# A two-layer decoder trunk on one core: first tiles and first weight chunk in smaller parts, identity made on chip

## The chip, the cores and the metric

The kernel runs on one core of one Trainium2 chip. The metric is device time in microseconds of one execution. Engines: TensorE (PE; PEld is its weight load), VectorE (DVE), ScalarE (ACT), GpSimd (POOL), SyncE (SP, which here only issues DMAs).

## The reference

Two layers work on 256 tokens of 1024 numbers, all in float32. Of each layer only the beginning matters here:

```python
def rmsnorm(x, g):
    xf = x.astype(jnp.float32)
    y = xf * lax.rsqrt(jnp.mean(xf * xf, axis=-1, keepdims=True) + EPS)
    return (y * g.astype(jnp.float32)).astype(x.dtype)
...
    h = rmsnorm(x, mix_norm)
    z = h @ w_in
...
    g = jax.nn.sigmoid((h @ w_branch_gate).astype(jnp.float32)).astype(x.dtype)
```

`z` goes to three token mixers (sparse, sliding-window and latent attention, with rotary tables made from the positions); their outputs are weighted by the gates, merged and multiplied by `w_out`; a gated feed-forward part of 2816 columns and a gated embedding part follow. After the second layer comes a last norm.

## The kernel before

The tokens are two tiles `t` of 128. A multiplication, `lin(name)`, takes the transposed tokens as the stationary and 512 columns of weights as the moving operand. For accuracy each float32 operand is split into a rounded part (high) and a residual (low), and each contraction step of 128 rows makes three products into one bank of PSUM: high x high, high x low, low x high. Weights come in chunks of two contraction steps (512 KB). A chunk is loaded by SyncE into one of four `raw` buffers, rounded by ScalarE into `wh` (the cast `wh<-raw`), and VectorE makes the residual `wl`; there are six pairs of `wh` and `wl`. `upper` issues the cast, its inner `rest` the residual and then the load of the chunk four further on.

The first multiplication of layer 0 is `gc0` (gate columns of mixer C, chunks 0 to 3), the second `g1` (chunks 4 to 7). `gc0` goes through its eight contraction steps in blocks of two, tile 0 then tile 1 in each block; `g1` makes all eight steps of tile 0, then those of tile 1. The two banks of `gc0` are read by ScalarE as gates, `gateC = tanh(z * rh)`, where `rh` is half the inverse root of the mean square of the tile's tokens, computed on GpSimd from sums that ScalarE makes (`junk<-x`, the squares).

The split tokens `hT` are made so: four 128x128 transposes on TensorE (`tr<-con,x`, with the identity in the constants `con`), a product with the norm's gain on VectorE (`xg<-tr,lp`, the gain in the loaded parameters `lp`), the rounding on ScalarE (`hT<-xg`), the residual on VectorE. `parts(t, g)` does this for tile `t` and half `g` of the 1024 features. Warm-up products on a tile of ones (`pv<-wrm`, counts in `WARM`) stand between.

The order on each engine is that of issue in the program. Most of it is set by a planner, `W`, that keeps estimated times of the engines and takes waiting pieces of work from a queue by due time; `feed` issues casts and residuals of coming chunks by these estimates. The first steps are written out by hand at the end of `build`, and `script[t, k]` puts pieces of them ahead of step `k` of tile `t` of `gc0`. The program builds the rotary tables on the side: GpSimd reduces the angles (`kq`, `kp`, `ang`), VectorE makes one step (`kq<-kq,ang`), ScalarE evaluates sines, for which it loads another function table (`ACT_TABLE_LOAD`) and afterwards the one with tanh again.

Each DMA counts on one of eight semaphores in turn, and the order below names them (`DMAHW0` is the load of `con`).

Of the kernel before, what the change touches and what calls it, by code (L numbers as in the profile page):

```python
# [8 lines left out]
F32 = mybir.dt.float32  # L9
F32R = mybir.dt.float32r  # L10
BF16 = mybir.dt.bfloat16
I32 = mybir.dt.int32
AF = mybir.ActivationFunctionType
# [49 lines left out]
LEAD, GAP = 128, 256  # L63


C_ID, C_FREQ, C_FIRST = 0, 128, 176
C_CB, C_CM, C_MV, C_S, C_J, C_N = 0, 32, 64, 192, 224, 228
C_BAND, C_CAUS, C_ALL = 0, 128, 256

# [148 lines left out]
def build(tc, wst, xin, pin, posn, cst, lpar, fnorm, out):  # L218
# [34 lines left out]
    def load_to(n):  # L253
        while st["dma"] < min(n, len(CHUNKS)):
            i = st["dma"]
            off, kk, c = CHUNKS[i]
            r = sb([P, 1024], name="raw", bufs=RAWB, p=wp)
            nc.sync.dma_start(out=r[:, :kk * c],
                              in_=wst[off:off + P * kk * c].rearrange("(p n) -> p n", p=P))
            W.op("D", kk * c * P * 4 / 350e3, [r.tensor.name], [])  # L260
            W.end[r.tensor.name] = ("D", W.t["D"] + 2.0)
            raws[i] = r
            st["dma"] += 1
# [67 lines left out]
    def lin(l, name, nk, lhs, evac, blocks=None, wait=0.0, halves=False):  # L331
# [5 lines left out]
        for b in blocks:  # L337
            for t in range(2):
                if t and halves:
                    break  # L340
                for k in range(k0, k0 + b):
                    for fn in script.pop((t, k), ()):
                        fn()
                    i, wh, wl = wtile(l, name, k)
                    xh, xl = lhs(t, k)
                    o = banks[t][:, :c]
                    T.matmul(out=o, lhsT=xh, rhs=wh, start=(k == 0), stop=False)
                    T.matmul(out=o, lhsT=xh, rhs=wl, start=False, stop=False)
                    T.matmul(out=o, lhsT=xl, rhs=wh, start=False, stop=(k == nk - 1))
                    if k == nk - 1:  # L350
                        evac(t, banks[t])
                    if t == 1 and (k % kp == kp - 1 or k == nk - 1):
                        done(i, wait if k0 + b == nk else 0.0)
                    W.tick()
            k0 += b
# [20 lines left out]

    x = [[sb([P, 512], name=f"x{t}{g}") for g in range(2)] for t in range(2)]
    con = sb([P, C_FIRST], name="con")
    con2 = sb([P, C_N], name="con2")
    pos = sb([P, 2], I32, name="pos")  # L380
    lps = {}
# [15 lines left out]
    mload = sb([P, 2, P], name="mload", tag="kall", bufs=3)  # L397
    load(nc.gpsimd, mload, cst[:, C_FIRST + C_N:].rearrange("p (a b) -> p a b", a=2))
    load(nc.gpsimd, con2, cst[:, C_FIRST:C_FIRST + C_N])
    ident = con[:, C_ID:C_ID + P]  # L400
    identb = sb([P, P], BF16, name="identb")
    identr = sb([P, P], F32R, name="identr")
    masks = sb([P, 2, P], BF16, name="masks")
# [861 lines left out]
        return n4  # L1265


    nm = Norm(lps[0][:, L_MIX:L_MIX + 8])
    wrm = sb([P, 512], BF16, name="wrm", tag="junk")
    V.memset(wrm, 1.0)  # L1270
    wps = ps("pv")
# [24 lines left out]
    def split(i):  # L1296
# [2 lines left out]
            upper(i)  # L1299
        return late.get(i, lambda: None)  # L1300

    def start_1():
        nm.square(0, 0)
        nm.square(1, 0)
        w2 = split(2)
        lo = parts(0, 1)
        w2()
        lo()

    def start_2():  # L1310
        w3 = split(3)
        lo = parts(1, 1)
        w3()
        lo()
        w4 = split(4)
        nm.square(0, 1)
        w4()
# [2 lines left out]
        W.push([], setup_masks, 20.0)  # L1320
        split_to(HLB)

    warm(WARM[0])
    lo = parts(0, 0)
    w0 = split(0)
    lo()
    warm(WARM[1])
    lo = parts(1, 0)
    w0()
    warm(WARM[2])  # L1330
    w1 = split(1)
    lo()
    w1()
    script[1, 0] = [start_1]
    script[0, 2] = [start_2]
    for l in range(DEPTH):
        nm = layer(l, nm, None)
    W.until(lambda: len(sent) == 2)
# [3 lines left out]
SPACE = 4.4  # L1342
SLACK = 0.9
TWO = "ga"
WARM = (7, 4, 4)
NEAR = 2
WAIT = 1.5

# [1 line left out]
def host_layout(inputs):  # L1350
# [47 lines left out]
    lp = np.ascontiguousarray(np.stack(lp))  # L1398
    i = np.arange(P)
    con, con2, con3 = (np.zeros((P, n), np.float32) for n in (C_FIRST, C_N, C_ALL))  # L1400
    con[:, C_ID:C_ID + P] = np.eye(P)
    con3[:, C_CAUS:C_CAUS + P] = np.where(i[None, :] <= i[:, None], 0, NEG)
    con3[:, C_BAND:C_BAND + P] = np.where(i[None, :] > i[:, None], 0, NEG)
    fr = [10000.0 ** (-np.arange(0, d, 2) / d) for d in (64, 32)]
# [34 lines left out]
```

## Time and profile before

| | |
|---|---|
| median of 3 runs | 967.37 us (967.33 to 967.55) |
| the profiled execution | 968.79 us, of which 967.0 us is the span from the first to the last instruction |
| instructions | 13566 |
| mean granted TensorE clock | 0.997 of 2.4 GHz |

The page gives each engine's busy time as a share of the span. Matmuls are pipelined, and the end of each is modelled, so that a product's printed duration is longer than the distance to the next one. A row's "idle" is the time in which the engine did nothing ahead of the instruction, and the name behind the arrow is what ended it. All times are microseconds from the span's start unless marked ns. Almost every instruction carries line 214, the helper through which the program issues; so rows are told apart by their tiles.

### The profile page before, as it was taken

Reading aid. Unit: us, or ns where it says so; the run is one execution under the profiler, and the core shown is the slowest. Engines: PE = TensorE matmul, PEld = TensorE weight load, DVE = VectorE, ACT = ScalarE, POOL = GpSimd, SP = SyncE. Lnnn points to the kernel's source line nnn. Section 1 sums busy time; section 2 is a strip of 40 time slices with the busy share of each in tenths; the row PEclk is TensorE's granted clock in tenths of the full one; section 3 lists DMA queues with packets and bytes.
Section 4 is the critical chain, followed back from the end, with each engine's and each line's share of the span. In section 5 each row is a group of like instructions: output and inputs, shape, how many; then the busy total and the mean of one; then the engine's idle time right before and its main releaser. Section 6 shows DMA issues by size and latency. Waiting matters only on the chain.

```text
span 967.0 us, 13566 instructions
## 1 busy us (share of the span) xinstructions
PE 954.5 (99%) x4915; PEld 785.3 (81%) x4915; DVE 665.5 (69%) x1044; ACT 555.2 (57%) x1013; POOL 51.0 (5%) x101
## 2 busy tenths in 40 slices
PE   8999999999999999999999999999999999999996
PEld 5888887777888888888888898877788888888886
DVE  6696798668776666655767868866786766666554
ACT  6668766565554445443665686666655544444444
POOL 7200000000010000000121000000000000000010
PEclk9999999999999999999999999999999999999999
DMA  8556534424555555656454664443444555555551
GB/s 281 163 164 227 182 110 153 152 87 162 175 184 186 199 182 175 196 174 209 158 173 156 201 204 142 131 153 131 131 139 167 194 189 193 192 189 180 190 175 44
DMA packets 46595, 164.29 MB, mean 170 GB/s; under 512 B 5504, under 2 KB 5760, under 8 KB 46528
## 3 DMA queue, kind: packets, MB, share of 16 engines
q1 hardware_dynamic: 45648, 161.80, 50.9%
q0 software_dynamic: 448, 1.30, 0.4%
q8 instruction: 39, 0.64, 0.3%
q10 hardware_dynamic: 432, 0.32, 0.1%
q14 instruction: 28, 0.23, 0.1%
HBM read 162.35 MB, written 1.05 MB: 169 GB/s over the span
## 4 chain that ended last, share of the span: by engine, by line
PE 97%; DVE 1%; ACT 1%; DMA 1%; issue 0%; ACTq 0%; DVEq 0%
PE lin L214 81%; PE tr L214 7%; PE sc L214 5%; PE pv L214 3%; PE hidps L214 2%; DMA lp<-lpar 1%; DVE wl L214 0%; DVE um L214 0%; ACT xf L214 0%; DVE khA L214 0%; DVE U L214 0%; ACT dup L214 0%; ACT ctok L214 0%; ACT kTC L214 0%; ACT gat L214 0%
## 5 line engine op out<-in xcount | busy, mean ns | idle before, releaser
L214 PE MATMUL lin<-wh,hT 128*128 128x512 f32 (+2 forms) x1600 | 512.6, 389 | 0.3 <-ACT wh L214 0.3
L214 DVE TENSOR_TENSOR wl<-raw,wh 128x1024 fp32r<-128x1024 f32 (+2 forms) x308 | 369.3, 1208 | 88.1 <-ACT wh L214 81.7
L214 ACT CAST wh<-raw 128x1024 fp32r<-128x1024 f32 (+2 forms) x308 | 317.2, 1037 | 134.4 <-PE lin L214 126.1
L214 PEld LDWEIGHTS lin<-wh,hT 128*128 128x128 f32 x1600 | 297.9, 189 | 55.4 <-issue 0.8
L214 PE MATMUL lin<-wl,hT 128*128 128x512 f32 (+2 forms) x800 | 305.8, 382 | 1.3 <-DVE wl L214 1.3
L214 PEld LDWEIGHTS lin<-wl,hT 128*128 128x128 f32 x800 | 151.1, 189 | 26.7 <-DVE wl L214 1.6
L214 PE MATMUL lin<-wh,hd 128*128 128x512 f32 x352 | 110.9, 392 | 0.0
L214 PEld LDWEIGHTS lin<-wh,hd 128*128 128x128 f32 x352 | 66.1, 188 | 13.6
L214 PE MATMUL lin<-wl,hd 128*128 128x512 f32 x176 | 68.5, 389 | 0.0
L214 PE MATMUL lin<-wh,oT 128*128 128x512 f32 x192 | 64.6, 397 | 0.0
L214 ACT ACTIVATE th<-lin,rh 128x256 f32<-128x256 f32 (+1 forms) x52 | 26.2, 504 | 65.4 <-PE lin L214 65.3
L214 ACT ACTIVATE p<-sc,negm 128x256 f32<-128x256 f32 (+1 forms) x128 | 52.6, 426 | 2.8 <-DVE negm L214 2.8
L214 DVE SCALAR_TENSOR_TENSOR th<-th,lin 128x256 f32<-128x256 f32 x44 | 18.4, 417 | 49.5 <-ACT th L214 49.5
L214 DVE TENSOR_REDUCE negm<-sc 128x2 f32<-128x512 f32 (+1 forms) x48 | 33.0, 687 | 27.6 <-PE sc L214 27.3
L214 ACT COPY pT<-tr 128x512 f32<-128x512 f32 x48 | 28.1, 584 | 36.4 <-PE tr L214 36.1
L214 PEld LDWEIGHTS lin<-wh,oT 128*128 128x128 f32 x192 | 36.1, 188 | 7.8 <-issue 0.8
L214 PE MATMUL lin<-wh,mT 128*128 128x512 f32 x128 | 41.5, 395 | 0.0
L214 POOL TENSOR_SCALAR n0v<-ssq 128x1 f32<-128x1 f32 x7 | 2.1, 304 | 706.0 <-ACT junk L214 705.9
L214 PEld LDWEIGHTS lin<-wl,hd 128*128 128x128 f32 x176 | 33.1, 188 | 6.6
L214 PE MATMUL lin<-wl,oT 128*128 128x512 f32 x96 | 37.5, 391 | 0.0
L214 DVE TENSOR_TENSOR xg<-tr,lp 128x512 f32<-128x512 f32 x28 | 19.3, 689 | 26.3 <-PE tr L214 20.9
L214 ACT CAST hd<-tr 128x256 fp32r<-128x256 f32 x44 | 16.2, 367 | 33.6 <-PE tr L214 33.6
(207 smaller groups left out, 1025.9 us busy)
## 6 DMA issues: line engine op xcount, KB each, us to landing
raw<-wst SPq DMA_DIRECT2D x296, 512.0 KB, 4.0
raw<-wst SPq DMA_DIRECT2D x8, 312.0 KB, 2.9
raw<-wst SPq DMA_DIRECT2D x4, 384.0 KB, 3.4
x<-xin SPq DMA_DIRECT2D x4, 256.0 KB, 5.8
w<-lpar POOLq DMA_DIRECT2D x2, 256.0 KB, 3.5
pr<-pin POOLq DMA_DIRECT2D x2, 256.0 KB, 3.8
fn<-fnorm SPq DMA_DIRECT2D x1, 512.0 KB, 3.2
out<-xf SPq DMA_DIRECT2D x2, 256.0 KB, 2.0
```

Source lines behind the costliest of these rows:

```text
L214: return fn(*a, **k)
```

## The change

The identity is made on GpSimd (a memset and a select) ahead of its DMA issues, and the 128 identity columns leave `con`, which now holds the gain of the first norm in 8 columns beside the 48 rotary frequencies. Chunk 0 is loaded in two DMAs of 256 KB and rounded in two halves, one for each contraction step. The first half of the features of both tiles is no longer multiplied by the gain into a buffer: ScalarE writes the rounded part with the gain as its scale, VectorE the residual from the transposes directly, each in pieces of 128 columns. In `gc0` of layer 0 the product low x high comes ahead of high x low. The second tile's transposes stand behind the first contraction step, the pieces of the start move to other steps, the squares of the first halves move from the first such piece to the third, and 10 warm-up products remain of 15.

```diff
--- before.py
+++ after.py
@@ -63,7 +63,7 @@
 LEAD, GAP = 128, 256
 
 
-C_ID, C_FREQ, C_FIRST = 0, 128, 176
+C_GAIN, C_FREQ, C_FIRST = 0, 8, 56
 C_CB, C_CM, C_MV, C_S, C_J, C_N = 0, 32, 64, 192, 224, 228
 C_BAND, C_CAUS, C_ALL = 0, 128, 256
 
@@ -255,8 +255,9 @@
             i = st["dma"]
             off, kk, c = CHUNKS[i]
             r = sb([P, 1024], name="raw", bufs=RAWB, p=wp)
-            nc.sync.dma_start(out=r[:, :kk * c],
-                              in_=wst[off:off + P * kk * c].rearrange("(p n) -> p n", p=P))
+            src = wst[off:off + P * kk * c].rearrange("(p n) -> p n", p=P)
+            for o in (slice(0, c), slice(c, kk * c)) if i == 0 else (slice(0, kk * c),):
+                nc.sync.dma_start(out=r[:, o], in_=src[:, o])
             W.op("D", kk * c * P * 4 / 350e3, [r.tensor.name], [])
             W.end[r.tensor.name] = ("D", W.t["D"] + 2.0)
             raws[i] = r
@@ -345,8 +346,9 @@
                     xh, xl = lhs(t, k)
                     o = banks[t][:, :c]
                     T.matmul(out=o, lhsT=xh, rhs=wh, start=(k == 0), stop=False)
-                    T.matmul(out=o, lhsT=xh, rhs=wl, start=False, stop=False)
-                    T.matmul(out=o, lhsT=xl, rhs=wh, start=False, stop=(k == nk - 1))
+                    pair = ((xh, wl), (xl, wh))
+                    for x_, w_ in pair[::-1] if c0 == 0 else pair:
+                        T.matmul(out=o, lhsT=x_, rhs=w_, start=False, stop=(k == nk - 1 and (x_ is xl) == (c0 != 0)))
                     if k == nk - 1:
                         evac(t, banks[t])
                     if t == 1 and (k % kp == kp - 1 or k == nk - 1):
@@ -376,6 +378,10 @@
 
     x = [[sb([P, 512], name=f"x{t}{g}") for g in range(2)] for t in range(2)]
     con = sb([P, C_FIRST], name="con")
+    ident = sb([P, P], name="ident")
+    G.memset(ident, 0.0)
+    G.affine_select(out=ident, in_=ident, compare_op=ALU.not_equal, fill=1.0, base=0, pattern=[[-1, P]],
+                    channel_multiplier=1)
     con2 = sb([P, C_N], name="con2")
     pos = sb([P, 2], I32, name="pos")
     lps = {}
@@ -397,7 +403,6 @@
     mload = sb([P, 2, P], name="mload", tag="kall", bufs=3)
     load(nc.gpsimd, mload, cst[:, C_FIRST + C_N:].rearrange("p (a b) -> p a b", a=2))
     load(nc.gpsimd, con2, cst[:, C_FIRST:C_FIRST + C_N])
-    ident = con[:, C_ID:C_ID + P]
     identb = sb([P, P], BF16, name="identb")
     identr = sb([P, P], F32R, name="identr")
     masks = sb([P, 2, P], BF16, name="masks")
@@ -1265,7 +1270,7 @@
         return n4
 
 
-    nm = Norm(lps[0][:, L_MIX:L_MIX + 8])
+    nm = Norm(con[:, C_GAIN:C_GAIN + 8])
     wrm = sb([P, 512], BF16, name="wrm", tag="junk")
     V.memset(wrm, 1.0)
     wps = ps("pv")
@@ -1299,19 +1304,72 @@
             upper(i)
         return late.get(i, lambda: None)
 
+    def tr_x(t):
+        b = ps("tr")
+        for k in range(4):
+            transpose(b[:, k * P:(k + 1) * P], x[t][0][:, k * P:(k + 1) * P])
+        return b, nm.place(t, 0)
+
+    def hi_x(bo, ks):
+        for k in ks:
+            S.activation(out=bo[1][:, 0, k], in_=bo[0][:, k * P:(k + 1) * P], func=AF.Copy, scale=nm.gain[:, k:k + 1])
+
+    def lo_x(bo, ks):
+        for k in ks:
+            V.scalar_tensor_tensor(out=bo[1][:, 1, k], in0=bo[0][:, k * P:(k + 1) * P], scalar=nm.gain[:, k:k + 1],
+                                   in1=bo[1][:, 0, k].bitcast(F32), op0=ALU.mult, op1=ALU.subtract)
+
+
+
+    warm(WARM[0])
+    x0 = tr_x(0)
+    r0 = raws.pop(0)
+    st["split"] = 1
+    hls[0] = h0, l0 = tuple(sb([P, 1024], F32R, name="w" + p, tag=f"w{p}0") for p in "hl")
+    near, far = (0, 1), (2, 3)
+
+    def half_hi(h):
+        S.copy(out=h0[:, h], in_=r0[:, h])
+
+    def half_lo(h):
+        V.tensor_tensor(out=l0[:, h], in0=r0[:, h], in1=h0[:, h].bitcast(F32), op=ALU.subtract)
+
+    first, second = slice(0, 512), slice(512, 1024)
+    hi_x(x0, near)
+    half_hi(first)
+    lo_x(x0, near)
+    half_lo(first)
+    half_hi(second)
+    half_lo(second)
+    hi_x(x0, far)
+    nm.ok.add((0, 0))
+    warm(WARM[1])
+
     def start_1():
-        nm.square(0, 0)
-        nm.square(1, 0)
+        x1 = tr_x(1)
+        hi_x(x1, near)
+        lo_x(x1, near)
+        lo_x(x0, far)
+        load_to(RAWB + 1)
+        w1 = split(1)
+        w1()
+        hi_x(x1, far)
+        lo_x(x1, far)
+        nm.ok.add((1, 0))
+
+    def start_2():
         w2 = split(2)
         lo = parts(0, 1)
         w2()
         lo()
 
-    def start_2():
+    def start_3():
         w3 = split(3)
         lo = parts(1, 1)
         w3()
         lo()
+        nm.square(0, 0)
+        nm.square(1, 0)
         w4 = split(4)
         nm.square(0, 1)
         w4()
@@ -1320,19 +1378,9 @@
         W.push([], setup_masks, 20.0)
         split_to(HLB)
 
-    warm(WARM[0])
-    lo = parts(0, 0)
-    w0 = split(0)
-    lo()
-    warm(WARM[1])
-    lo = parts(1, 0)
-    w0()
-    warm(WARM[2])
-    w1 = split(1)
-    lo()
-    w1()
-    script[1, 0] = [start_1]
+    script[0, 1] = [start_1]
     script[0, 2] = [start_2]
+    script[1, 2] = [start_3]
     for l in range(DEPTH):
         nm = layer(l, nm, None)
     W.until(lambda: len(sent) == 2)
@@ -1342,7 +1390,7 @@
 SPACE = 4.4
 SLACK = 0.9
 TWO = "ga"
-WARM = (7, 4, 4)
+WARM = (7, 3)
 NEAR = 2
 WAIT = 1.5
 
@@ -1398,7 +1446,7 @@
     lp = np.ascontiguousarray(np.stack(lp))
     i = np.arange(P)
     con, con2, con3 = (np.zeros((P, n), np.float32) for n in (C_FIRST, C_N, C_ALL))
-    con[:, C_ID:C_ID + P] = np.eye(P)
+    con[:, C_GAIN:C_GAIN + 8] = lp[0][:, L_MIX:L_MIX + 8]
     con3[:, C_CAUS:C_CAUS + P] = np.where(i[None, :] <= i[:, None], 0, NEG)
     con3[:, C_BAND:C_BAND + P] = np.where(i[None, :] > i[:, None], 0, NEG)
     fr = [10000.0 ** (-np.arange(0, d, 2) / d) for d in (64, 32)]
```

ScalarE's head, from its first DMA issue on, before (with what each row waits for; DVE, PE: counts of these engines; DMAHW1 to 7: loads of tokens and chunks):

```order
L373 DMA con<-cst 128x176
L373 DMA lp<-lpar 128x68
L214 ACT_TABLE_LOAD
L214 CAST hT<-xg 128x4x128 [waits DVE_49]
L214 CAST wh<-raw 128x1024 [waits DMAHW3_49]
L214 CAST hT<-xg 128x4x128 [waits DVE_49]
```

and with the change:

```order
L375 DMA con<-cst 128x56
L375 DMA lp<-lpar 128x68
L214 ACT_TABLE_LOAD [waits DMAHW0_49]
L214 ACTIVATE hT<-tr,con 128x128 [waits PE_49]
L214 ACTIVATE hT<-tr,con 128x128
L214 CAST wh<-raw 128x512 [waits DMAHW3_49]
L214 CAST wh<-raw 128x512 [waits DMAHW4_49]
```

The wait for the load of `con` (DMAHW0) now stands ahead of the table load, because the first activation takes its scale from `con`.

ScalarE further on, before: from the cast of chunk 4 to those of chunks 8 and 9. The squares (`junk,ssq`) are those of the second halves of the features; the casts behind them are those of chunks 5 and 6 together, of 7 between the two table loads, and of 8 and 9 together.

```order
L214 CAST wh<-raw 128x1024
L214 ACTIVATE junk,ssq_135<-x_104 128x512
L214 ACTIVATE junk,ssq_136<-x_106 128x512
L214 CAST wh<-raw 128x1024 x2
L214 ACT_TABLE_LOAD
L214 ACTIVATE cs<-kq 128x96
L214 ACTIVATE cs<-ang 128x96
L214 CAST wh<-raw 128x1024
L214 ACT_TABLE_LOAD
L214 ACTIVATE gateC<-lin,rh_314 128x512
L214 ACTIVATE gateC<-lin,rh_329 128x512
L214 CAST wh<-raw 128x1024 x2
```

With the change, from the second square of the first halves to the casts of chunks 7, 8 and 9; the casts ahead of them are chunk 4, and 5 and 6 together.

```order
L214 ACTIVATE junk,ssq_142<-x_105 128x512
L214 CAST wh<-raw 128x1024
L214 ACTIVATE junk,ssq_141<-x_104 128x512
L214 ACTIVATE junk,ssq_142<-x_106 128x512
L214 CAST wh<-raw 128x1024 x2
L214 ACTIVATE gateC<-lin,rh_340 128x512
L214 ACT_TABLE_LOAD
L214 ACTIVATE cs<-kq 128x96
L214 ACTIVATE cs<-ang 128x96
L214 ACT_TABLE_LOAD
L214 ACTIVATE gateC<-lin,rh_349 128x512
L214 CAST wh<-raw 128x1024 x3
```

The cast of chunk 7 moved from ahead of both gates to behind both, one gate moved ahead of the sines, and the four squares now lie around chunk 4's cast, where the first two were ahead of chunk 2's.

## Rows read from the trace of the kernel before

**Rows 1.** The page: busy time of the engines with its share of the span and the number of instructions, and the chain of work that ended last, by engine.

```profile
PE 954.5 (99%) x4915; PEld 785.3 (81%) x4915; DVE 665.5 (69%) x1044; ACT 555.2 (57%) x1013; POOL 51.0 (5%) x101
...
PE 97%; DVE 1%; ACT 1%; DMA 1%; issue 0%; ACTq 0%; DVEq 0%
```

**Rows 2.** The waits of TensorE from 26 us to the end: who waited for whom, microseconds in total, times, the longest.

```profile
PE sc L214 <- ACT kTC L214: 0.7, 2, 0.4
PE tr L214 <- ACT dup L214: 0.4, 2, 0.2
```

**Rows 3.** The chain that ended last, from 0 to 26 us: start, duration, what.

```profile
1.17 4.96 DMA lp<-lpar
```

**Rows 4.** TensorE in order of time, 8 to 29 us: start, duration, operation, output and operands, count, and in brackets the idle time ahead of it with what ended it. The row at 15.73 is the residual product of the fifth contraction step of the first multiplication (`gc0`), the one at 28.01 that of the seventh step of the second (`g1`), both of the first token tile.

```profile
8.58 0.50 PE L214 MATMUL lin<-wh,hT 128*128 128x512 f32 x1 [0.27 <-ACT wh L214]
10.35 0.50 PE L214 MATMUL lin<-wl,hT 128*128 128x512 f32 x1 [1.27 <-DVE wl L214]
...
15.73 0.40 PE L214 MATMUL lin<-wl,hT 128*128 128x512 f32 x1
...
28.01 0.39 PE L214 MATMUL lin<-wl,hT 128*128 128x512 f32 x1
```

**Rows 5.** Stretches of the start: length, TensorE's busy time and instructions, its granted clock (1.00 is 2.4 GHz, 0.50 is 1.2 GHz), busy share of the DMA engines, GB/s.

```profile
8.20:11.60 3.40, 1.85 (x7) 1.00 1.04 411
11.00:12.00 1.00, 1.00 (x6) 0.84 1.03 393
12.00:15.00 3.00, 3.00 (x10) 0.50 0.89 329
15.00:16.00 1.00, 1.00 (x8) 0.95 0.59 127
```

**Rows 6.** ScalarE in order of time, 19 to 29 us: start, duration, operation. `wh<-raw` is the rounding of a weight chunk, here chunk 7; `cs` are the sines of the rotary tables; `gateC` are the sigmoid gates of the two tiles.

```profile
22.56 0.28 ACT L214 ACTIVATE cs<-kq 128x96 f32<-128x96 f32 x1
22.75 0.27 ACT L214 ACTIVATE cs<-ang 128x96 f32<-128x96 f32 x1
22.93 1.03 ACT L214 CAST wh<-raw 128x1024 fp32r<-128x1024 f32 x1
23.97 1.28 ACT L214 ACT_TABLE_LOAD   x1
25.27 1.27 ACT L214 ACTIVATE gateC<-lin,rh 128x512 f32<-128x512 f32 x2
```

**Rows 7.** GpSimd in order of time, 9 to 25 us. `kq`, `kp`: reduction of the rotary angles; `n0y`, `rh`: the inverse root of tile 0 and its half.

```profile
9.30 1.31 POOL L214 TENSOR_SCALAR kp<-kq 128x96 f32<-128x96 f32 x1
...
17.80 0.61 POOL L373 DMA_DIRECT2D w<-lpar  x1
19.61 0.26 POOL L214 TENSOR_SCALAR kq<-kq 128x96 f32<-128x96 f32 x1 [1.19 <-DVE kq L214]
...
20.36 1.71 POOL L214 TENSOR_TENSOR n0y<-n0v,half 128x1 f32<-128x1 f32 x1
22.16 1.10 POOL L214 TENSOR_SCALAR rh<-n0y 128x1 f32<-128x1 f32 x1
```

**Rows 8.** VectorE in order of time, 18 to 29 us: the last step of the rotary angles, and the residual of chunk 7.

```profile
19.27 0.24 DVE L214 TENSOR_TENSOR kq<-kq,ang 128x96 f32<-128x96 f32 x1
...
23.99 1.23 DVE L214 TENSOR_TENSOR wl<-raw,wh 128x1024 fp32r<-128x1024 f32 x1 [0.82 <-ACT wh L214]
```

**Rows 9.** DMA issues, the first two from the stretch 0.70 to 0.74 us, the third from 2.1 to 4.67 us (chunks 1 and 2): queue, count, KB each, median microseconds from issue to landing.

```profile
x<-xin SPq DMA_DIRECT2D x1, 256.0 KB, 3.7
con<-cst ACTq DMA_DIRECT2D x1, 88.0 KB, 3.9
...
raw<-wst SPq DMA_DIRECT2D x2, 512.0 KB, 6.8
```

**Rows 10.** Issues of loads in order of time, 0.7 to 5 us: start, duration of the issue, queue.

```profile
0.73 0.39 SPq L373 DMA_DIRECT2D x<-xin  x1
0.73 0.41 ACTq L373 DMA_DIRECT2D con<-cst  x1
...
2.11 0.43 SPq L258 DMA_DIRECT2D raw<-wst  x1
...
4.66 0.33 SPq L258 DMA_DIRECT2D raw<-wst  x1
```

**Rows 11.** Groups of instructions of the whole kernel by line, engine, operation and form: count, then busy time and mean nanoseconds of one, then idle time ahead of them and what ended it.

```profile
L214 ACT ACTIVATE p<-sc,negm 128x128 f32<-128x128 f32 x64 | 22.7, 374 | 0.0
...
L214 ACT ACTIVATE junk<-x 128x512 bf16<-128x512 f32 x27 | 17.0, 628 | 19.3 <-DVE x L214 19.2
L214 DVE TENSOR_TENSOR hT<-xg,hT 128x512 fp32r<-128x512 f32 x24 | 16.9, 703 | 5.5 <-ACT hT L214 5.5
...
L214 ACT CAST hT<-xg 128x512 fp32r<-128x512 f32 x24 | 14.8, 618 | 26.6 <-DVE xg L214 26.6
...
L214 ACT ACTIVATE gateC<-lin,rh 128x512 f32<-128x512 f32 x8 | 5.4, 686 | 1.9 <-PE lin L214 1.9
L214 POOL TENSOR_TENSOR n0y<-n0v,half 128x1 f32<-128x1 f32 x7 | 5.4, 765 | 0.6
...
L214 POOL COPY ctok<-kpe 128x128 f32<-128x128 f32 x8 | 4.2, 542 | 62.2 <-ACT ctok L214 47.9 <-ACT gat L214 14.3
...
L214 POOL TENSOR_SCALAR rh<-n0y 128x1 f32<-128x1 f32 x6 | 2.2, 373 | 0.5
```

## The prediction

> **What bounds the kernel now.** I read the page first: TensorE is busy in 99% of the span and the chain that ended last is 97% TensorE [rows 1]. The waits of TensorE after 26 us come to 1.1 us in the whole kernel [rows 2]. From there on the program is one stream of products, and whatever moves the stream at 26 us moves its end by as much. So the question is at which time one and the same product is issued before and after. Beyond about the first hundred rows of each engine's order the two programs issue the same instructions in the same order, so nothing else can differ.
>
> The chain of waits up to 26 us [rows 3] shows what the start hangs on first: the load of `lp`, until 6.13 us; no longer piece stands ahead of the stream. The order of time on TensorE [rows 4] shows the same from its side: first product at 8.58, nothing until 10.35, and products every 0.227 us from 15.4 us on (18 steps of three products from 15.73 to 28.01 us: 12.28 / 54). In between the granted clock falls to 0.50, that is 1.2 GHz, from within 11:12 to within 15:16 us, after a stretch (8.2 to 11.6) in which TensorE was busy for only 1.85 of 3.4 us [rows 5]. Read as shares of full clock, the dip lasts (1-0.84)/0.5 + 3.0 + (1-0.95)/0.5 = 3.4 us.
>
> One more view matters, the order of time on the other engines from 17 to 28 us [rows 6 to 8]. ScalarE rounds chunk 7 (the cast at 22.93) before it loads the table for the gates (23.97) and evaluates both gates (25.27). TensorE wants the residual of chunk 7 at 28.01 us, the seventh contraction step of `g1`, first tile; that residual starts on VectorE at 23.99 and takes 1.2 us [rows 8]. So in this kernel chunk 7 is some 2.8 us early.
>
> **The start, step by step.** All times here are estimates, chained from durations in the rows.
>
> `x00` lands at 0.73+3.7 = 4.4 us and `con`, 88 KB, at 0.73+3.9 = 4.6 [rows 9, 10]; with 28 KB I take 4.5. The identity on GpSimd is not in the trace. Its two instructions cost between nothing and twice the slowest 128x96 operation, 2.6 us [rows 7]; the nearest row by shape is the 128x128 copy, 0.54 [rows 11], so 1.1 us together, from about 0.9. It is ready at 2.0 (0.9 to 3.5), before `x00`, and costs the transposes nothing. It delays what GpSimd does behind it; that price is below.
>
> The gain now comes from `con`, so `lp`'s 6.13 leaves the chain. But ScalarE's first table load now stands behind the wait for `con` (the order shows it; no row has a load held like that). Held, it ends at 4.5+1.28 = 5.8 us; free, it would be over before the transposes end at 5.2. I take it as held, since an engine takes its order one by one; the other case makes the first product 0.6 earlier and, because of what follows, nothing else. Two gain products of 128x128 (0.37 each by the nearest row) and half a chunk's cast (0.62) [rows 11] give the first product at 7.0 us instead of 8.58.
>
> Then data sets the pace. Two half residuals (0.70 each) end at 7.7 and 8.4. Chunk 1 lands at 2.11+6.8 = 8.9 [rows 9, 10]; behind the second tile's gains its cast (1.03) ends at 10.1 and its residual (1.23) at 11.4 [rows 6, 8]. Chunk 2 lands at 4.66+6.8 = 11.5: cast to 12.5, the cast of the first tile's second half to 13.1, residuals on VectorE to 13.7 and 14.3. The second tile's second half: gain 15.0, cast 15.7, chunk 3's residual 16.2, its own 16.8. There TensorE has waited some 1.1 us; 17 products of `gc0` are left, 17 x 0.227 = 3.9, and `g1` begins at 20.7. Before, it began 19 products ahead of 28.01: 23.70. Up to here the change is worth -3.0 us.
>
> Edits that cost nothing: the fifth DMA issue on SyncE (0.4 us) and the later issue of `x11` and chunk 3 (which now wait for `con` and `lp`, some 1.1 us later by my estimate) lie under DMA engines that are full up to 12 us [rows 5], with earlier data queued until chunk 2 lands; uncovered they would cost 0.4 and 1.1. The five warm-up products that go stood in waits. The half-size DMAs move the same bytes.
>
> **What is late next.** The order of ScalarE puts four things in front of chunk 7's cast: the gate of tile 0, a table load, two sines, a table load, the gate of tile 1. Ahead it had only the sines and one load, and no gate. The gate of tile 0 waits for `rh` of tile 0 from GpSimd, so chunk 7 now waits for GpSimd.
>
> When does `rh` come? ScalarE: cast at 15.7, two squares (0.63 each, and a read of the sum) to 17.1 [rows 11], chunk 4's cast to 18.1; VectorE: its residual to 19.3, `kq` to 19.5. Before, VectorE's `kq` began at 19.27 and GpSimd's at 19.61 [rows 7, 8]: the early start of TensorE doesn't reach this chain, because the squares now stand ahead of chunk 4. From GpSimd's `kq` to the end of `rh` it took 19.61 to 23.26 = 3.65 us, so 19.55+3.65 = 23.2. GpSimd itself is free for `kq` at 18.4 (its last DMA issue, 17.80+0.61) plus 1.1 for the identity, 19.5: just covered.
>
> From there ScalarE alone: gate 0.69 (23.9), table load 1.28 (25.2), sines 0.47 (25.7), table load 1.28 (27.0), gate 0.58 to the next start (1.27 for two less 0.69; 27.6), cast of chunk 7 1.03 (28.6); then VectorE's residual 1.23, 29.9 with 0.03 for each hand-over [rows 6, 8, 11]. TensorE is at this step at 20.7+18 x 0.227 = 24.8. It waits 3.8 us for the cast, makes one product, waits 1.0 us for the residual and goes on at 29.9, where before it was at 28.01: **+1.9 us**. The whole -3.0 is gone.
>
> Bounds: with the power and the half of it at their means over the kernel, 0.77 and 0.37 [rows 11], for the 1.71 and 1.10 they took here [rows 7], `rh` is there at 21.5 and the product comes 1.7 earlier: +0.2. If VectorE's chain comes 0.5 later, or the identity takes its 2.6 (1.5 more than is covered), it is +2.4 to +3.4.
>
> **The clock.** The idle stretch of 8.58 to 10.35 was enough for a fall [rows 4, 5]; here TensorE stands nearly still from 24.8 to 29.9. I take one dip like the one before, 3.4 us at half speed, all of it in work: 3.4/2 = **+1.7 us**. Bounds: nothing, where the low stretch falls into the wait itself, and 2.7, where it lasts 5.4 us from 29.9 (two such stretches, less what the wait covers). The old dip at 11.7 is in the 23.70 that the -3.0 is counted from; should it come in the new start too, the wait hides it.
>
> Sum: +1.9+1.7 = +3.6 us. The profiled execution took 968.79 (span 967.0 and 1.8 around it), which is 1.42 above the median 967.37; on the median 971.0, on the profiled execution 972.4. Later waits don't take it back: `rh` and the tables are there when their readers come, and 1.1 us of waits are all there is to shrink.
>
> **Rivals.** (a) *The clock doesn't pay*: chunk 7 is late as above but the low stretch falls into the wait, or `rh` comes at its early bound: +0.2 to +1.9, 967.6 to 969.3. For it: where the stretch falls is chance. Against: a wait of 5 us leaves little room for a full recovery inside. (b) *The gain survives* (faster): `rh` early enough that chunk 7 isn't missed. By the same chain the product comes 6.7 us after `rh`; break-even is at `rh` 21.3, the whole -3.0 needs 18.3. At `rh` 20.3, a gain of 1 us: 966.4; at best 964.4. For it: the chain ahead of `kq` hangs on chunk 2's landing, which could come earlier with 60 KB less ahead of it. Against: 60 KB are 0.2 us at the 411 GB/s of [rows 5], and the early bound above is 21.5. (c) *A table load costs more than its row*, since the engine must run empty around it: bounded by the row itself, up to 1.28 us more for each of the two ahead of chunk 7: 971.0+2.6 = 973.6. Against: around the load at 23.97 there is no such gap; the cast ahead of it runs 22.93 to 23.96 and the gate starts 0.02 us after it ends [rows 6]. The Trainium skill, "ScalarE: Activation LUTs", section "What ACT_TABLE_LOAD costs", speaks for it: a switch to another set costs the load, about 1283 ns, and a drain of about 1380 ns. By the page's figure the two loads would add an estimated 2.8 us to the sum. (d) *Nothing to see*: the start gains what the gates lose, within 0.5 us of 967.4; it needs both an early `rh` and no dip.
>
> **How the numbers follow.** Forecast (late chunk 7 and a dip) 0.67; (a) 0.17; (b) 0.08; (c) 0.04; (d) 0.04. A measurement of this kernel tells about 0.2%, 1.9 us, from no change. Faster by more: most of (b), 0.06. Within: nearly all of (a), (d) and the rest of (b), 0.21. Slower: 0.73. The forecast's own range is +1.9+0.8 to +2.8+2.3, 970.1 to 972.5. For 8 in 10 it reaches down through (a), to 968.0, and up to both bounds of the clock and `rh` together, 973.3.
>
> **What would show it.** First product near 7.0 (6.4 to 7.6), the first table load starting where `con` lands, `g1`'s first product at 20.5 to 22.5. Then in ScalarE's order of time: the gate of tile 0 at 22 to 24 released by GpSimd, two table loads, chunk 7's cast near 27.6; on TensorE two waits, on ScalarE's `wh` (3 to 4 us) and on VectorE's `wl` (1 us), and 1.2 GHz behind them. I am wrong if TensorE shows no wait over 1 us between 20 and 31 us; if the cast of chunk 7 begins before 25; or if the clock stays at 2.4 GHz after it.

## The result and the profile after

The changed kernel takes 972.39 us (median of 4 executions, 971.81 to 972.84) against 967.35 in the same session (967.2 to 967.55): a ratio of 1.0052, with a 95% interval of 1.0034 to 1.0069. It is 5.0 us slower. The profiled execution took 971.81 us, with a span of 970.0, 3.0 more than that of before. The result lies in the stated range and on the forecast side; the size was forecast as +3.6.

The page of the changed kernel: busy times, and the chain that ended last. The busy times answer to [rows 1]; TensorE's share in the chain fell from 97% to 94%.

```profile
PE 955.1 (98%) x4910; PEld 784.8 (81%) x4910; DVE 665.0 (69%) x1049; ACT 556.9 (57%) x1020; POOL 49.8 (5%) x103
...
PE 94%; DVE 2%; ACT 2%; issue 1%; DMA 0%; POOL 0%; ACTq 0%; DVEq 0%
```

The waits of TensorE from 26 us to the end, as in [rows 2]: the last three rows come to 0.4 us or less at a time, as before; the first two are new and long, and they follow each other at one place.

```profile
PE lin L214 <- ACT wh L214: 1.9, 1, 1.9
PE lin L214 <- DVE wl L214: 0.8, 1, 0.8
PE sc L214 <- ACT kTC L214: 0.7, 2, 0.4
PE tr L214 <- ACT dup L214: 0.4, 2, 0.2
PE tr L214 <- DVE p L214: 0.3, 2, 0.2
```

That place in TensorE's order of time, with the first product and the one long wait of the start (answers to [rows 4]). The row at 29.07 is the product that stood at 28.01.

```profile
7.00 0.73 PE L214 MATMUL lin<-wh,hT 128*128 128x512 f32 x2 [0.68 <-ACT wh L214]
...
17.67 0.50 PE L214 MATMUL lin<-wh,hT 128*128 128x512 f32 x1 [0.77 <-DVE hT L214]
...
25.51 0.39 PE L214 MATMUL lin<-wh,hT 128*128 128x512 f32 x1
27.82 0.50 PE L214 MATMUL lin<-wh,hT 128*128 128x512 f32 x1 [1.92 <-ACT wh L214]
29.07 0.50 PE L214 MATMUL lin<-wl,hT 128*128 128x512 f32 x1 [0.76 <-DVE wl L214]
```

ScalarE over the same time (answers to [rows 6]), with the first table load ahead of it. The gate of tile 0 waits 0.45 us for `rh` from GpSimd; then come a table load, the sines, a table load, the other gate, and only at 26.73 the cast of chunk 7, the first of the three in the last row.

```profile
4.52 1.28 ACT L214 ACT_TABLE_LOAD   x1 [4.52 <-DMA con<-cst]
...
22.38 0.69 ACT L214 ACTIVATE gateC<-lin,rh 128x512 f32<-128x512 f32 x1 [0.45 <-POOL rh L214]
23.08 1.28 ACT L214 ACT_TABLE_LOAD   x1
24.37 0.28 ACT L214 ACTIVATE cs<-kq 128x96 f32<-128x96 f32 x1
24.56 0.27 ACT L214 ACTIVATE cs<-ang 128x96 f32<-128x96 f32 x1
24.85 1.28 ACT L214 ACT_TABLE_LOAD   x1
26.14 0.69 ACT L214 ACTIVATE gateC<-lin,rh 128x512 f32<-128x512 f32 x1
26.73 2.93 ACT L214 CAST wh<-raw 128x1024 fp32r<-128x1024 f32 x3
```

And the clock behind the wait (answers to [rows 5]; the columns are the same). The old fall at 11.7 us is gone; 1.2 GHz now lasts (1-0.82)/0.5 + 3.0 + (1-0.97)/0.5 = 3.4 us from 29.6 us on, all of it in work.

```profile
25.74:28.84 3.10, 0.66 (x2) 1.00 0.48 188
29.00:30.00 1.00, 0.93 (x3) 0.82 0.00 0
30.00:33.00 3.00, 3.00 (x8) 0.50 0.88 268
33.00:34.00 1.00, 1.00 (x8) 0.97 0.86 317
```

### The profile page after: what moved, and what is told of

It is laid out like the page before. It is cut to its first block, busy times and chain, and to the rows that moved or that the text cites. A ratio compares the mean times of both kernels' runs of the same rounds, so it can differ in the third digit from the quotient of the medians.

```text
span 970.0 us, 13571 instructions
## 1 busy us (share of the span) xinstructions
PE 955.1 (98%) x4910; PEld 784.8 (81%) x4910; DVE 665.0 (69%) x1049; ACT 556.9 (57%) x1020; POOL 49.8 (5%) x103
## 4 chain that ended last, share of the span: by engine, by line
PE 94%; DVE 2%; ACT 2%; issue 1%; DMA 0%; POOL 0%; ACTq 0%; DVEq 0%
PE lin L214 79%; PE tr L214 6%; PE sc L214 5%; PE pv L214 3%; PE hidps L214 2%; DVE wl L214 1%; ACT L214 0%; DMA con<-cst 0%; DVE um L214 0%; ACT wh L214 0%; DVE hT L214 0%; ACT xf L214 0%; DVE khA L214 0%; ACT junk L214 0%; DVE p L214 0%
## 5 line engine op out<-in xcount | busy, mean ns | idle before, releaser
L214 DVE TENSOR_TENSOR wl<-raw,wh 128x1024 fp32r<-128x1024 f32 (+3 forms) x309 | 369.1, 1204 | 89.9 <-ACT wh L214 83.5
L214 ACT CAST wh<-raw 128x1024 fp32r<-128x1024 f32 (+3 forms) x309 | 317.2, 1034 | 135.7 <-PE lin L214 126.0
L214 DVE TENSOR_TENSOR p<-p,sm 128x512 f32<-128x512 f32 x48 | 33.2, 692 | 2.1
```

Source lines behind the costliest of these rows:

```text
L214: return fn(*a, **k)
```

## Experiments

Times are medians; "the product" is the residual product of `g1`'s seventh step, first tile, at 28.01 us in [rows 4]. Each run is compared with executions of before from its own session (medians 967.4 to 967.5). A line of three dots in a code cut stands for lines that are left out.

**1. Is it the place of chunk 7's cast?** The changed kernel, with that cast forced ahead of the first gate:

```diff
+    def through(i):
+        while st["split"] <= i:
+            st["split"] += 1
+            upper(st["split"] - 1)
     script[0, 1] = [start_1]
+    script[0, 6] = [lambda: through(7)]
```

> The changed kernel with one instruction moved: ScalarE's cast of chunk 7 stands ahead of the first gate, behind the cast of chunk 6; nothing else in any order differs. Theory 1 (the loss is this cast's place in ScalarE's order, and the clock's fall that the wait brings): the cast starts near 21.95, TensorE has no wait over 0.3 us from 19 to 31 us, the residual product of g1's seventh step, first tile, comes at 25.7 instead of 29.07, the clock stays at 2.4 GHz behind it, and the time falls by 3.3+1.7 = 5.0 us, to 966.8 to 967.4. Rival 2 (the late rh is what counts: whatever waits for the gates, the banks of PSUM above all, is late next): a wait of 2 us or more turns up on the gates between 24 and 33 us and the time stays above 970. Rival 3 (the clock falls anyway, from the waits of the new start): no wait, but 0.50 in some stretch, 968.5 to 969.

Measured: 968.18, ratio 1.0008 (0.9999 to 1.0018), so 4.2 us of the loss are gone; the forecast of 966.8 to 967.4 missed by the rest. The product comes at 26.06, without a wait, and no fall of the clock follows. But rival 2 has its share: ScalarE reaches the gate of tile 1 at 26.92, two casts stand behind it, and the copy `zc` of `g1`'s first tile comes late.

```profile
26.92 0.69 ACT L214 ACTIVATE gateC<-lin,rh 128x512 f32<-128x512 f32 x1
27.51 1.98 ACT L214 CAST wh<-raw 128x1024 fp32r<-128x1024 f32 x2
29.39 0.69 ACT L214 ACTIVATE zc<-lin,n0y 128x512 f32<-128x512 f32 x1
```

```profile
30.14 0.66 PE L214 MATMUL tr<-ident,zc 128*128 128x128 f32 x4 [1.42 <-ACT zc L214]
```

**2. What does the clock cost?** The changed kernel with 8+4 products that nobody reads (on the operands of the step before) in the two waits:

```diff
+                    if (l, name, t, k) == (0, "g1", 0, 6):
+                        fill(*was, FILL[0])
                     i, wh, wl = wtile(l, name, k)
...
                     T.matmul(out=o, lhsT=xh, rhs=wh, start=(k == 0), stop=False)
+                    if (l, name, t, k) == (0, "g1", 0, 6):
+                        fill(*was, FILL[1])
+                    was = xh, wh
...
+FILL = (8, 4)
```

> The changed kernel with 12 more products on TensorE whose results nobody reads: 8 ahead of the product that waits for chunk 7's cast and 4 ahead of the one that waits for its residual, 12 x 0.227 = 2.7 us of work in 3.1 us of waiting. Chunk 7 stays late. Theory 1 (the standing still makes the clock fall, and that costs 1.7 us beyond the wait): the residual product stays at 29.1, the clock stays at 2.4 GHz from 28 to 34 us, and the time falls by 1.7 us, to 970.1 to 970.7. Rival (the fall has another cause, or such products do not prevent it): 0.50 again from about 29.6 to 33, time unchanged at 971.8 to 972.4.

Measured: 970.05 (969.87 to 970.62), ratio 1.0027 (1.0016 to 1.0038). The product stays at 29.08, and the clock stays up:

```profile
25.66:29.00 3.34, 3.15 (x14) 1.00 0.35 140
29.00:34.00 5.00, 5.00 (x26) 1.00 0.69 224
```

So on the medians the fall costs 972.39-970.05 = 2.3 us, more than the 1.7 of the one profiled execution. The remaining 970.05-967.41 = 2.6 us are the wait itself.

**3. Is the fall always the same?** The changed kernel once more, unchanged.

> The changed kernel, unchanged, once more. Its four executions had 971.81 (the profiled one, mean granted clock 0.996) and 972.4 to 972.8 (0.994). If the fall behind the late chunk 7 is in every execution, all come again between 971.5 and 973, and the profile shows the residual product at 29.1 and 1.2 GHz for 3.4 us behind it. If the fall is a matter of chance, as the added table copy suggests (the same 3.1 us of waiting without a fall in its profile, 970.6), some executions lie near 970.1, and the median between 970.1 and 972.4.

Measured: 971.89 (970.25 to 972.74, 5 executions), ratio 1.0044 (1.0031 to 1.0057). Both readings hold in part: by their times most executions have the fall, and one (970.25) stands where the run without a fall stands. Against this median the fall costs 971.89-970.05 = 1.8 us, so 2.3 is not to be taken to the tenth. In the profiled one, 972.74, the low stretch is twice as long, (1-0.87) x 3.3/0.5 + 0.2 + 5.0 + (1-0.61)/0.5 = 6.8 us from 27.9 us on, of which 0.9 lie in the wait:

```profile
25.50:28.80 3.30, 0.68 (x2) 0.87 0.43 169
29.00:34.00 5.00, 5.00 (x13) 0.50 0.70 231
34.00:35.00 1.00, 1.00 (x6) 0.61 0.02 8
```

Half of the low stretch that lies in work is thus 1.7 us in one execution and 3.0 in the other; by their times against 970.05 they lose 1.8 and 2.7, and the execution at 970.25 loses 0.2, for the same wait.

**4. What does the profiled execution of before stand for?** Before, unchanged:

> The kernel before, unchanged, timed and profiled once more; the ratio is 1.000 by definition. It settles what the profiled execution of before (968.79) stands for against its median (967.35). Theory A (the fall of TensorE's clock between 11.7 and 15.1 us is not in every execution): executions near 967.3 show no such stretch, their mean granted clock is higher than the 0.997 of the profiled one by about 1.7/967 = 0.002, and the seventh contraction step of g1, first tile, comes 1.2 to 1.7 us before 28.01. Theory B (the fall is always there and the 1.4 us lie in the tail or in the landings): the clock is 0.50 again from about 12 to 15 us, the product stands at 28.0, and a difference in time lies behind the last product.

Measured: 967.41, ratio 1.0003 (0.9994 to 1.0012). The profiled execution is again a long one, 969.21, with 1.2 GHz from 11.6 to 15.1 us and the product at 28.14; that shows the fall again, but not what the others do. So before, with 5 products that nobody reads in the 1.27 us wait of [rows 4]:

```diff
                     T.matmul(out=o, lhsT=xh, rhs=wh, start=(k == 0), stop=False)
+                    if (l, c0, t, k) == (0, 0, 0, 0):
+                        fill(xh, wh, 5)
...
```

> The kernel before with 5 more products (1.1 us) on TensorE, whose results nobody reads, in the 1.27 us in which it waits for the residual of chunk 0 (between 8.58 and 10.35 us); no other row changes. They are meant to keep the clock from falling at 11.7 us. Theory A (the two profiled executions of before, 968.79 and 969.21, hold a fall of the clock that most executions near 967.4 do not have): the median stays at 967.4 within 0.3 us, while the profiled execution comes down to 967 to 967.6, has 2.4 GHz from 10 us on, and its residual product of g1's seventh step, first tile, at 26.2 to 26.6 instead of 28.0. Theory B (every execution of before has that fall): the median falls by 1.7 us, to 965.7.

Theory A, in every number: the median doesn't move (967.43, ratio 0.9999, 0.9990 to 1.0007), the profiled execution comes down to 967.23, 2.4 GHz holds, and the product stands at 26.23.

```profile
10.00:12.00 2.00, 1.86 (x11) 1.00 1.03 418
12.00:16.00 4.00, 4.00 (x21) 1.00 0.86 283
```

```profile
26.23 0.39 PE L214 MATMUL lin<-wl,hT 128*128 128x512 f32 x1
```

By their times, then, most executions of before have no fall. The start that the prediction measured from, 28.01, carried 1.8 us that the median doesn't have.

**5. The reverse of experiment 1, on before.** One instruction moved, chunk 7's cast behind both gates:

```diff
     def feed():
...
+            if i == 7 and not st.get("gated"):
+                break
...
                 S.activation(out=gt[:, t, :], in_=b, func=AF.Tanh, scale=nm.rh[t])
+                st["gated"] = t
```

> The kernel before with one instruction moved: ScalarE's cast of chunk 7 stands behind both gates instead of ahead of the second table load. From the rows of before the table load then starts at 22.9, the gates at 24.2, the cast at 25.4, and the residual ends at 27.6. Theory A (ordinary executions want this residual near 26.3): TensorE waits some 0.3 us for the cast and 1.0 us for the residual, 968.7, and up to 2.3 us more where the clock falls behind that; the profiled execution, where it wants the residual at 28.0, shows no wait there and keeps its time. Theory B (the residual is wanted at 28.0 in every execution, so chunk 7 has 2.8 us to spare): 967.4, nothing changes. Rival to the whole reading (the place of this one cast is without effect): 967.4 as well, but in both kinds of execution and with the product near 26.3 in some.

Measured: 968.84, ratio 1.0014 (1.0006 to 1.0023): +1.36 for theory A's +1.3. Here the profiled execution happens to be one without the fall at 11.7 us, and it shows both waits, with the cast at 25.38 as worked out:

```profile
25.38 2.93 ACT L214 CAST wh<-raw 128x1024 fp32r<-128x1024 f32 x3
```

```profile
26.47 0.50 PE L214 MATMUL lin<-wh,hT 128*128 128x512 f32 x1 [0.18 <-ACT wh L214]
27.73 0.50 PE L214 MATMUL lin<-wl,hT 128*128 128x512 f32 x1 [0.76 <-DVE wl L214]
```

The place of this one instruction is enough to make the kernel before slower. It had 1.0 us to spare there (26.23 against a residual that is ready at 25.2 in [rows 8]), not 2.8.

**6. The parts called free.** The identity alone on before (its lines are those of the change), and on the changed kernel a table load that need not wait:

```diff
+    S.activation(out=small(1, "tab0"), in_=wrm[:, 0:1], func=AF.Copy, scale=1.0)
```

> The kernel before with one part of the change: the identity is made on GpSimd and the 128 identity columns leave the load of the constants; the gain still comes from the parameters' load, no other order changes. Forecast (a part that costs nothing): the two instructions on GpSimd take 0.5 us together and are over at 1.3, before the tokens land; the first product stays at 8.6, set by the parameters' load at 6.1, and the time at 967.4 within 0.4. Rival 1 (smaller load, earlier data): every landing behind it 0.1 to 0.2 sooner, 967.2. Rival 2 (the delay of GpSimd's own DMA issues and angles by 0.5 us reaches rh and the gates): up to 0.5 later, 967.9.

> The changed kernel with one more instruction on ScalarE, ahead of everything else: a one-column copy of the tile of ones, so that the first table load need not wait for the load of the constants. It would then run from 1.4 to 2.7 us, and the gain activations start when the transposes end. Forecast: first product 0.5 to 0.7 us sooner (6.3 to 6.5), and no change at the end, since chunk 7's cast still waits behind the gate of tile 0, and that on rh: residual product of g1's seventh step at 29.1, 972.4 within 0.5. Rival (what the start gains goes through, because rh too hangs on the start): 0.6 sooner everywhere, 971.8. Rival 2: a longer standing still ahead of 29.1 moves the clock's fall; up to 0.6 either way.

Identity: 967.94, ratio 1.0005 (0.9996 to 1.0014), which can't be told from no change. But it misses the forecast of 967.4 within 0.4 and stands where rival 2 put it (967.9): its 11 executions begin at 967.85, above the 967.48 that is the median of before. So a cost of some 0.5 us is neither shown nor excluded. Its two instructions are over at 1.29 us (0.21 and 0.29 us, where 1.1 was assumed).

The table load indeed starts at 1.65 when nothing holds it, and the first product comes at 6.53. The product doesn't come sooner (29.53), as forecast; but the time is 970.54 (969.86 to 972.27), ratio 1.0033 (1.0022 to 1.0045), and the forecast of 972.4 missed. Its profile has the same 2.02+0.76 us of waits and no fall behind them:

```profile
26.00:29.50 3.50, 0.75 (x3) 1.00 0.37 142
29.60:36.00 6.40, 6.40 (x30) 1.00 0.62 184
```

Why this program mostly escapes the fall and the changed kernel mostly doesn't, no run here tells; in time its wait lies 0.4 us later.

**7. Towards a faster version.** The squares of the first halves in ScalarE's idle stretches:

```diff
@@ start_1
         nm.ok.add((1, 0))
+        nm.square(0, 0)
@@ start_3
         w3 = split(3)
+        nm.square(1, 0)
         lo = parts(1, 1)
         w3()
         lo()
-        nm.square(0, 0)
-        nm.square(1, 0)
```

> The changed kernel with the squares of the two first halves in ScalarE's idle stretches instead of ahead of chunk 4's cast: that of tile 0 behind the second tile's roundings (idle from 10.9 to 11.9), that of tile 1 behind chunk 3's cast (idle from 14.6 to 15.7). The planner then puts chunk 7's cast between the sines and the second table load, ahead of both gates, as in the kernel before. Theory 1: rh of tile 0 comes 1.0 to 1.5 us sooner (near 21.1), chunk 7's cast starts near 22.3, no wait over 0.3 us on TensorE from 19 to 31 us, no fall of the clock behind it, time 966.8 to 967.6. Rival (the squares delay chunk 2's cast or the second half of tile 1, and the start gives the gain back): the cast of chunk 2 at 12.2 or later, g1's seventh step at 26.2 or later, 967.5 to 968.5.

Measured: 967.27 (966.56 to 968.11), ratio 0.9998 (0.9990 to 1.0007): the loss is gone, and nothing is won. The product comes at 26.01, the cast of chunk 7 at 22.36 and `zc` in time. `rh` didn't come sooner (22.24, for 22.35): GpSimd's power took 1.58 us here and 0.57 in the changed kernel. It was the order on ScalarE that helped, not `rh`.

Then the second halves of the features in the new form too, with and without three more warm-up products:

```diff
-        lo = parts(0, 1)
+        x2 = tr_x(0, 1)
+        hi_x(x2, near + far, 1)
...
-        lo = parts(1, 1)
+        x3 = tr_x(1, 1)
+        hi_x(x3, near + far, 1)
...
```

> An attempt at a faster version on top of the run with the early squares: the second halves of the features take the form that the change gave the first halves (ScalarE rounds with the gain as its scale in 4 pieces, VectorE makes the residual in 4 pieces), and ScalarE's order from the sines to the gates is held as it was in that run. VectorE, busy without a break from 9.6 to 18 us, saves 0.69+0.75 for 4 x 0.26 of each tile, 0.8 us in all; ScalarE takes 1.0 us more, of some 1.5 idle. If VectorE sets the pace of the start, the 0.68 us wait for tile 1's residual at 17 us goes and the time is 966.5 to 966.8 against 967.27. Rival (ScalarE or the landings set it): a wait for a chunk's cast instead, 967.0 to 967.5.

> The same with 3 more warm-up products (0.65 us) in TensorE's wait for chunk 0's cast (0.7 to 1.4 us, ending at 7.0). They can delay the first product by no more than what the wait is shorter than 0.65. If the spread of the early-squares run (966.56 to 968.11) comes from falls of the clock that this wait brings in some executions, the upper end comes down to 967 and the median falls by 0.2 to 0.5 against the run without them; if not, both medians agree within 0.2.

Measured: 968.29 (ratio 1.0010, 1.0001 to 1.0019) and 968.38 (1.0011, 1.0002 to 1.0020); the added products do nothing. The start gains what was meant, the product comes at 25.46, but `zc` is 1.54 us late. The trace puts this down to one step on GpSimd, for which the sines wait 0.96 us; no run took that step's delay away, so this cause is argued, not shown:

```profile
19.87 2.77 POOL L214 TENSOR_SCALAR kq<-kq 128x96 f32<-128x96 f32 x1 [2.72 <-DVE kq L214]
```

```profile
20.43 1.28 ACT L214 ACT_TABLE_LOAD   x1
22.68 0.28 ACT L214 ACTIVATE cs<-kq 128x96 f32<-128x96 f32 x1 [0.96 <-POOL kq L214]
```

The last run moves the step that this one waits for ahead of chunk 4's residual:

```diff
+        rope_t["last"]()
         w4 = split(4)
         nm.square(0, 1)
         w4()
         nm.square(1, 1)
-        rope_t["last"]()
```

> The scaled run without added warm-up products, with one instruction moved: VectorE's last step of the rotary angles stands ahead of chunk 4's residual instead of behind it. In the scaled run GpSimd's next step, 0.26 to 0.30 us elsewhere, took 2.77 (19.87 to 22.64) and ended when VectorE's two residuals did (22.51), ScalarE waited 0.96 us for it with the sines, and TensorE 1.54 us for the copy zc behind the gates. Theory (GpSimd is held while VectorE works without a break, and the start's gain is lost there): VectorE's step at 17.3, GpSimd's over by 19.7 even if it is held through chunk 4's residual, the sines not late, the wait for zc under 0.3 us, 966.5 to 967.0. Rival (GpSimd's steps for rh are held instead, behind chunks 5 and 6): rh of tile 0 still after 23.5, a wait of 1 us or more for zc, 967.8 to 968.4.

Measured: 968.35 (ratio 1.0010, 1.0001 to 1.0020), nothing gained. GpSimd's step starts 1.0 us sooner and ends no sooner: it is held through chunk 4's residual, three small casts and the next two residuals, and ends 0.13 us behind them. The forecast of 966.5 to 967.0 missed: that GpSimd is held came out as expected, how long it is held did not. GpSimd, then VectorE:

```profile
18.85 3.91 POOL L214 TENSOR_SCALAR kq<-kq 128x96 f32<-128x96 f32 x1 [1.50 <-DVE kq L214]
```

```profile
18.67 1.22 DVE L214 TENSOR_TENSOR wl<-raw,wh 128x1024 fp32r<-128x1024 f32 x1
19.80 0.22 DVE L214 CAST identb<-ident 128x128 bf16<-128x128 f32 x1
...
20.28 2.35 DVE L214 TENSOR_TENSOR wl<-raw,wh 128x1024 fp32r<-128x1024 f32 x2
```

No version here is faster than the kernel before by more than can be told.

## Why the prediction held, and where its sizes were off

**Right: the mechanism.** What stood under "what would show it" is there: first product at 7.00 (7.0, though its terms as written, 5.8 and 2 x 0.37 and 0.62, add up to 7.2), the first table load 0.07 us behind the landing of `con` (4.45), `g1`'s first product at 21.65 (the product is the 20th, due at 25.51+2 x 0.227 = 25.96, less 19 x 0.227), the gate of tile 0 at 22.38 released by GpSimd, chunk 7's cast at 26.73 (27.6), two waits on `wh` and `wl`, and 1.2 GHz behind them. Experiments 1 and 5 show from both sides that the place of the cast is the cause. The pace of 0.227 us holds too; the row at 15.73, from which it is counted, is the fifth step in TensorE's order, that is the third contraction step of tile 0, 18 steps ahead of the one at 28.01.

**Wrong by 1.8: where the sum starts.** The sum compared the new 29.9 with 28.01 and put the difference on the median. The 1.42 us by which the profiled execution was longer were noted, but not asked about: they are the fall at 11.7 us, which that execution has and the median doesn't (experiment 4). Against 26.23 the wait costs 29.07-26.23 = 2.8 us, not 1.9.

**Wrong by 0.9: the pace of the start.** TensorE was to be at the step at 24.8 and was there at 25.74. The term is VectorE's chain: chunk 2 landed at 11.87 (11.5), and each of its pieces came later than chained, up to the residual of tile 1's second half, which ended at 17.62 (16.8):

```profile
12.97 1.25 DVE L214 TENSOR_TENSOR wl<-raw,wh 128x1024 fp32r<-128x1024 f32 x1
14.15 0.75 DVE L214 TENSOR_TENSOR hT<-xg,hT 128x512 fp32r<-128x512 f32 x1
15.00 0.69 DVE L214 TENSOR_TENSOR xg<-tr,con 128x512 f32<-128x512 f32 x1
15.61 1.22 DVE L214 TENSOR_TENSOR wl<-raw,wh 128x1024 fp32r<-128x1024 f32 x1
16.74 0.88 DVE L214 TENSOR_TENSOR hT<-xg,hT 128x512 fp32r<-128x512 f32 x1
```

So the new start is worth 26.23-25.96 = 0.3 us and not 3.0: of the 3.0, 1.8 were the fall in the profile of before, 0.9 this chain. That alone would have ruled out rival (b): there was hardly a gain to survive.

**Wrong by 0.9 the other way: `rh`.** It was ready at 22.35, not 23.2. `kq` on GpSimd began later (20.19 for 19.55), but the way from there to `rh` took 2.16 us where 3.65 had been carried over from [rows 7]: the power and the half took 0.57 and 0.70, nearer to their means [rows 11] than to 1.71 and 1.10. From `rh` to the product it was 6.7 us, as chained. Of TensorE's first wait of 1.92 us for a forecast of 3.8, one half is this and the other the slower start.

**The clock: right in place, a little small.** 1.7 us in the profiled execution, as forecast; 2.3 on this median and 1.8 on that of experiment 3. On the base of ordinary executions the terms are 2.8+2.3 = 5.1 us, for 5.0 measured.

**What was luck.** That 972.39 lies in the range, 0.1 us below its upper end, owes something to two errors of opposite sign. With the base put right but `rh` as late as forecast, the product would come 29.9-26.23 = 3.7 us later, and with the 2.3 of the clock the time would be 967.35+6.0 = 973.4 us, above the range of 970.1 to 972.5. The 972.4 of the prediction was said of the profiled execution, which took 971.81; that the median came to the same number is chance.

**The rivals.** (a), the clock doesn't pay, is what one execution of experiment 3 does by its time, but at 970.25 and not at the 967.6 to 969.3 put down for it: the wait alone costs 2.6 to 2.8 us. (c) falls: around both loads ahead of chunk 7 the engine stands for 0.01 or 0.02 us (22.38+0.69 to 23.08, 23.08+1.28 to 24.37, 24.56+0.27 to 24.85, 24.85+1.28 to 26.14), so they cost their row and no more. The Trainium skill, "ScalarE: Activation LUTs", section "What ACT_TABLE_LOAD costs", agrees on the load, 1283 ns; the drain of some 1380 ns that it adds is not in this trace. (d) needed an early `rh` and no fall, and had neither. The early table load gave nothing at the product, as claimed (29.53 for 29.07); that the identity cost nothing is not shown (experiment 6).

## What to carry over

A start that is made faster on one engine is worth what the last of its followers gets: follow the next few loads, too, through the order of the engines that issue in order, here a cast behind gates behind a table load. Before a sum is put on a median, ask what makes the profiled execution longer than it; 1.4 us were a fall of the clock that the median didn't have. And where TensorE must stand still, products that nobody reads in the wait separate the wait from what the clock adds, at no cost in time (the product behind them came at 29.08 for 29.07, experiment 2).

## What the runs showed of the hardware

A GpSimd step can be held through several instructions of VectorE: the same 128x96 step took 0.26 us in the kernel before [rows 7], 0.30 in the changed kernel, 2.77 and 3.91 in the scaled runs of experiment 7. The last two ran beside VectorE while that issued without a break, and each ended 0.13 us behind the last instruction of VectorE's stretch. The Trainium skill, "SBUF — State Buffer", section "SBUF: two separate sides", says that the two engines share a pair of ports as an exclusive lock: where VectorE's instruction has two inputs in SBUF and GpSimd's reads SBUF, or VectorE's runs in a mode that uses both ports, whichever starts first has the pair for the whole instruction, and the other stands still. The trace agrees that GpSimd stands still beside the residuals, which read `raw` and `wh`; but the step of 3.91 us stands through six instructions of VectorE in a row, not one.

This is not a rule that VectorE always keeps GpSimd out. In the kernel before, VectorE is busy without a break from 9.08 to 12.30 us, and two GpSimd steps are done inside that stretch, the one at 9.30 in [rows 7] (over at 10.61) and the next (over at 11.22); a third begins in it, at 11.30. What decides between the two cases no run here shows. VectorE, then GpSimd, before:

```profile
9.08 1.22 DVE L214 TENSOR_TENSOR wl<-raw,wh 128x1024 fp32r<-128x1024 f32 x1
10.21 0.75 DVE L214 TENSOR_TENSOR hT<-xg,hT 128x512 fp32r<-128x512 f32 x1
10.89 1.41 DVE L214 TENSOR_TENSOR wl<-raw,wh 128x1024 fp32r<-128x1024 f32 x1
```

```profile
10.70 0.52 POOL L214 TENSOR_TENSOR ang<-ang,kp 128x96 f32<-128x96 f32 x1
11.30 1.31 POOL L214 TENSOR_SCALAR kp<-kq 128x96 f32<-128x96 f32 x1
```

Nearly the same wait of TensorE, 2.7 to 2.8 us in two pieces with one product between, was followed by 0 (the early table load), 3.4 (the changed kernel) or 6.8 us (the same kernel again) at 1.2 GHz; a wait of 1.3 us at 9 us by some 3.4 us in two profiles of before and by none in that of experiment 5. So executions of one program can lie apart by more than their medians do: the nine of the changed kernel go from 970.25 to 972.84 us, while its two medians are 972.39 and 971.89.
